# A transformer block with a mixture of experts: the experts' feed-forward in two halves of 1792 columns instead of four quarters of 896

## The chip, the cores and the metric

The kernel runs on one core of one Trainium2 chip. The metric is the device time of one execution in microseconds (us). Five engines matter: TensorE (PE, with the weight loads shown as PEld), VectorE (DVE), ScalarE (ACT), GpSimd (POOL) and SyncE (SP), which issues the loads of the weights. All work in fp32, with products split in two parts.

## The reference

Two layers over 272 tokens (16 of them learned) with 1024 features: a mixer of pooling and differential attention, then a feed-forward. The first layer's feed-forward is dense, the second's a mixture of eight experts, of which each token goes to two:

```python
D_MODEL = 1024; SEQ = 256; D_FF = 3584; N_EXPERTS = 8; TOP_K = 2
def swiglu(h, wg, wu, wd):
    return (jax.nn.silu(h @ wg) * (h @ wu)) @ wd
def moe_swiglu(h, router, wg, wu, wd):
    ...
    out = jnp.zeros_like(h)
    for e in range(N_EXPERTS):
        out = out + combine[..., e:e + 1] * swiglu(h, wg[e], wu[e], wd[e])
    return out
```

After it come the residual and a last norm. Each expert's three matrices are 1024 x 3584, 1024 x 3584 and 3584 x 1024 floats, 44 MB; eight experts make 352 MB of weights that are read once.

## The kernel before, in words

**Dense part.** Until about 615 us the kernel runs the two mixers and the dense feed-forward. The change doesn't touch it.

**Blocks.** The mixture's weights come in blocks of about 1 MB, in the order of use. An expert is worked in `NS` = 4 steps of `SLAB` = 896 columns of the hidden dimension. A step has four blocks of the gate's matrix (256 rows x 896 columns, in SBUF 128 x 2 x 896, 896 KB), four of up's, and four of down's, which belong to the step before: three of 1 MB and one of 512 KB, since 896 rows are seven chunks of 128. `Weights.load` issues them on SP (L101) into raw buffers, as these come free.

**Two parts.** TensorE multiplies at its fast rate in a rounded format; so each block is taken in two parts. ACT copies the upper part, whi (`first_parts`, L149), three blocks ahead of use (`AHEAD`), into one of `NHI` = 7 slots. DVE subtracts it from the block, which gives wlo (`second_parts`, L157), one block ahead (two near the end), into one of `NLO` = 5 slots; with this the raw buffer is free and SP starts the next transfer. PE multiplies both parts with the tokens (`stream`, L1089): eight matmuls a block, 448 columns wide for gate and up, 512 for down.

**Tokens.** An expert has 128 places for tokens. With at most 64 tokens, the tokens' own lower parts lie in the other 64 places, and a fold at the end of each sum (`folded`: ACT copies the sum to part, L1060, and PE multiplies it with fold back into the sum, L1064) adds the two halves. With more than 64, the places are tokens, and the tokens' lower parts are multiplied in extra matmuls behind each pair of blocks (`unit`, under `tc.If(many > 0)`; L1185 for gate and up with exl, L1205 for down with hl).

**A step.** `up(E, "pgate")` sums the gate; after the second block of up the hook `gated` folds it and takes the Silu on ACT (L1210, L1212, gs). `up(E, "pup")` sums up; after the second block of down `product` folds it and multiplies on DVE (L1214, L1216). `down` multiplies the step before into y. `turn` transposes gs on PE (L1072, L1075), ACT copies it to hh (L1266), and `parts_of` makes hl on DVE (L1079, L1081). Hooks, `then(m, f)`, run f behind block m. PE's, ACT's and DVE's order is that of the code (`tc.manual_schedule`); a queue passes nothing.

**PSUM.** y has a pair of banks. All other sums rotate over three pairs.

**The end.** After an expert, `keep` scales y (ACT, L1095, yout) and POOL stores it to `ydram` (L1096). `rows(t)` gathers each token's two rows from `ydram` on POOL (L1136, into yout and exl), and DVE adds them to hsum (L1139). `rows(0)` is called at the end of the last expert's second step, its adds follow six blocks later.

Of the kernel before, what the change touches and what calls it, by code (L numbers as in the profile page):

```python
# [60 lines left out]
class Weights:  # L61
# [3 lines left out]
    def __init__(self, nc, blocks, slots):  # L65
        self.nc, self.blocks = nc, blocks
        self.free = []
        self.kept, self.keep = [], 0
        self.slots = slots
        self.raw = {}  # L70
        self.parts = {}
        self.order = [(b, i) for b, blk in enumerate(blocks) for i in range(blk[1])]
        self.n_split = 0
        self.n_load = 0
        self.first = next(b for b, blk in enumerate(blocks) if blk[2] is None)
        self.n_large = len(blocks) - self.first
        self.n_small = sum(blk[1] for blk in blocks[:self.first])
        self.n_hi = self.n_lo = 0
        self.his, self.los = {}, {}
        self.taken = 0  # L80
        self.second = None
# [63 lines left out]
    def first_parts(self, j):  # L145
        while self.n_hi < min(j + 1, self.n_large):
            w, shaped = self.large(self.n_hi)
            hi = shaped(self.slot(self.n_hi % NHI, f"whi{self.n_hi}"))
            self.nc.scalar.activation(hi, w, AF.Copy)  # L149
            self.his[self.n_hi] = hi  # L150
            self.n_hi += 1

    def second_parts(self, j):
        while self.n_lo < min(j + 1, self.n_large):
            w, shaped = self.large(self.n_lo)
            lo = shaped(self.slot(NHI + self.n_lo % NLO, f"wlo{self.n_lo}"))
            self.nc.vector.tensor_sub(lo, w, self.his[self.n_lo].bitcast(F32))  # L157
            self.los[self.n_lo] = lo
            self.freed(self.first + self.n_lo)
            self.n_lo += 1  # L160
# [3 lines left out]
def tile_block(ctx, tc, x, meta_tokens, rel_bias, w_in, pool_group_w, w_pool_up, w_attn_up, w_out, dense_w_gate,  # L164
# [68 lines left out]
    def add_up(w, e, s):  # L233
        for b in range(4):
            src = w[0, e, b * 256:b * 256 + 256, s * SLAB:(s + 1) * SLAB]
            blocks.append((src.rearrange("(k p) f -> p k f", p=P), 1, None))

    def add_down(e, s, c0, m):
        for b in range((NSC + 1) // 2):
            r = s * SLAB + b * 256  # L240
            n = min(2, NSC - 2 * b)
            src = moe_w_down[0, e, r:r + n * P, c0:c0 + m]
            blocks.append((src.rearrange("(p k) f -> p k f", k=n), 1, None))
# [724 lines left out]
    def places():  # L968
        nc.vector.scalar_tensor_tensor(posb, few[:, None].to_broadcast([P, 2, NE]), float(HALF), pos, op0=ALU.mult,
                                       op1=ALU.add)  # L970

    def tables(pc_):
# [4 lines left out]
        nc.vector.tensor_scalar(big2, few, -1.0, 1.0, op0=ALU.mult, op1=ALU.add)  # L977
# [24 lines left out]
    exl = act.tile([P, 2, NCH, CAP], F32R, name="exl", tag="xl")  # L1002

    class Expert:


        def __init__(self, e):
# [9 lines left out]
            self.xh, self.xl = exh[:, e % 2], exl[:, e % 2]  # L1017
# [5 lines left out]
        def gather(self, cs=range(NCH)):  # L1023
            if cs[0] == 0:
                self.pg = two("pgat").rearrange("p h (c s) -> p (h c) s", s=CAP)
# [5 lines left out]
        def first(self, cs=slice(0, NCH)):  # L1031
            nc.scalar.activation(self.xh[:, cs], self.pg[:, cs], AF.Copy)

# [6 lines left out]
        def scales(self):  # L1040
            self.pst = bank("pst")
# [13 lines left out]
    def folded(E, ps):  # L1055
# [6 lines left out]
        def add():  # L1062
            for hf in range(2):
# [3 lines left out]
    def chunk(ci):  # L1067

        b, i = ci // 2, ci % 2
        return slice(b * 256 + i, (b + 1) * 256, 2) if ci < NSC - 1 else slice(b * 256, SLAB)  # L1070

    def turn(hs):  # L1072
        pt = two("pth").rearrange("p h (c s) -> p (h c) s", s=P)[:, 0:NSC]
        for ci in range(NSC):
            nc.tensor.transpose(pt[:, ci], hs[:, chunk(ci)], ident)  # L1075
        return pt
# [77 lines left out]
    def unit(bs, run, extra, many):  # L1154

        held = []
        m0 = step[0]
        for b in bs:
            m = step[0]
            ws.first_parts(m + AHEAD)  # L1160
            ws.second_parts(m + (1 if m < ws.n_large - 10 else 2))
            held.append(ws.his.pop(m))
            run(b, (held[-1], ws.los.pop(m)))
            if b != bs[-1]:
                for f in hooks.pop(m, ()):
                    f()
                step[0] += 1
        with tc.If(many > 0):  # L1168
            for b, hi in zip(bs, held):
                extra(b, hi)  # L1170
        for f in hooks.pop(step[0], ()):
            f()
        step[0] += 1

    def up(E, name):
        ps = two(name)
        outs = [(ps[:, hf, 0:SW], slice(hf * SW, (hf + 1) * SW)) for hf in range(2)]

        def run(b, parts):
            stream(outs, parts, [E.xh[:, 2 * b], E.xh[:, 2 * b + 1]], b == 0, b == 3)  # L1180

        def extra(b, hi):
            for i in range(2):
                for o, f in outs:
                    nc.tensor.matmul(o, E.xl[:, 2 * b + i], hi[:, i, f], start=False, stop=True, skip_group_check=True)  # L1185

        for bs in ((0, 1), (2, 3)):
            unit(bs, run, extra, E.many)
        return ps[:, :, 0:SW]

    def down(E, s, h, hfs=(0, 1)):
# [4 lines left out]
        def chunks(b):  # L1196
            return range(2 * b, min(2 * b + 2, NSC))

        def run(b, parts):
            stream(outs, parts, [h[0][:, ci] for ci in chunks(b)], s == 0 and b == 0, s == NS - 1 and b == 3)  # L1200

        def extra(b, hi):
            for i, ci in enumerate(chunks(b)):
                for o, f in outs:
                    nc.tensor.matmul(o, h[1][:, ci], hi[:, i, f], start=False, stop=True, skip_group_check=True)  # L1205

        for bs in ((0, 1), (2, 3)):
            unit(bs, run, extra, E.many)

    def gated(E, pg_, gs2, add):  # L1210
        add()
        nc.scalar.activation(gs2, pg_, AF.Silu, scale=E.rc[:, 0:1])  # L1212

    def product(E, pu, gs2, add):  # L1214
        add()
        nc.vector.scalar_tensor_tensor(gs2, pu, E.rc[:, 0:1], gs2, op0=ALU.mult, op1=ALU.mult)  # L1216
# [7 lines left out]
    for e in range(NE):  # L1224
        for s in range(NS):
            end = e == NE - 1 and s == NS - 1
            m0 = step[0]
# [8 lines left out]
            pg_ = up(E, "pgate")  # L1236
            gs = mb.tile([P, SLAB], F32, name="gs")
            gs2 = gs.rearrange("p (h f) -> p h f", h=2)
            add_g = folded(E, pg_)
            then(m0 + 5, lambda E=E, pg_=pg_, gs2=gs2, add=add_g: gated(E, pg_, gs2, add))  # L1240
            pu = up(E, "pup")
            add_u = folded(E, pu)
            if prev is None:
                product(E, pu, gs2, add_u)
            else:
                then(m0 + (8 if end else 9), lambda E=E, pu=pu, gs2=gs2, add=add_u: product(E, pu, gs2, add))
                if end:
                    hh, hl = (x_[:, NE % 2, 0:NSC] for x_ in (exh, exl))

                    def last_turn():  # L1250
                        pt = turn(gs)
                        nc.scalar.activation(hh, pt, AF.Copy)
                        then(m0 + 10, lambda: parts_of(E, pt, hh, hl))

                    then(m0 + 9, last_turn)
                down(prev[0], prev[1], turned)
            if end:
                turned = (hh, hl)
                continue

            m1 = step[0]
            add_y = folded(prev[0], prev[0].y) if prev is not None and prev[1] == NS - 1 else None
            pt = turn(gs)
            hh = mb.tile([P, NSC, P], F32R, name="hh")
            hl = mb.tile([P, NSC, P], F32R, name="hl")
            nc.scalar.activation(hh, pt, AF.Copy)  # L1266
            turned = (hh, hl)
            then(m1, lambda E=E, pt=pt, hh=hh, hl=hl: parts_of(E, pt, hh, hl))
            if add_y is not None:
                then(m1, add_y)  # L1270
                then(m1 + 1, lambda E=prev[0]: keep(E, E.e))
            if e + 1 < NE:
                if s == 0:
                    then(m1 + 4, lambda e=e: (made.append(Expert(e + 1)), made[-1].folds()))
                elif s == 1:
                    made[-1].gather()
                    then(m1, made[-1].first)
                    then(m1 + 1, made[-1].second)
                elif s == 2:
                    made[-1].scales()  # L1280
                    then(m1, made[-1].scaled)
            elif s == 0:
                hsum = residual()
            elif s == 1:
                add = rows(0)
                then(m1 + 5, lambda add=add: (add(), added.append(rows(1))))
                then(m1 + 12, lambda: added[0]())
# [8 lines left out]
    def squares_of(t, hf):  # L1296
        sq = mb.tile([P, SLAB], F32, name="fsq", tag=("gs", "hh")[hf])[:, 0:512]
# [59 lines left out]
    with tc.If(most > CAP):  # L1357
        with tc.For_i(0, NE, 1) as ev:
# [29 lines left out]
            for j in range(NFB):  # L1388
# [26 lines left out]
                ho = mb.tile([P, SLAB], F32, name="ho", tag="hh")[:, 0:512]  # L1415
# [49 lines left out]
```

## Time and profile before

| | us |
|---|---|
| three runs | 1563.52, 1564.65, 1564.68 |
| median | 1564.65 |
| profiled execution, time | 1566.1 |
| profiled execution, span | 1564.3 |
| PE busy in it | 1469.2 (94%) |
| PE weight loads busy | 1277.6 (82%) |
| DVE busy | 1306.1 (83%) |
| ACT busy | 1072.1 (69%) |
| POOL busy | 20.2 (1%) |

The queue of the weights moves 449.97 MB in 177,328 packets. The busy shares are means over the whole span; the mixture, from about 616 us on, has to be read by stretches. A line such as "x4" in the timeline joins four instructions in a row; a matmul's end overlaps the next one's start, so the pace of PE is read from the distance of the starts. The bracket at a row's end tells how long the engine was idle before it and what released it.

### The profile page before, as it was taken

How to read it: one execution, taken by the hardware profiler on the slowest of the kernel's cores; microseconds unless marked ns; L12 is line 12 of the kernel's file. 1: busy time of each engine (PE TensorE's matmuls, PEld its weight loads, DVE VectorE, ACT ScalarE, POOL GpSimd, SP SyncE). 2: the span in 40 equal slices, each digit the busy share in tenths (PEclk: the TensorE clock that was granted, in tenths of full speed). 3: DMA queues.
4: the chain of work that ended last, by engine and by line, in shares of the span. 5: the costliest groups of instructions: out<-in, count | busy, mean ns of one | idle time of the engine just before them, and what ended most of it. 6: DMA issues, size and time to landing. Idle time of an engine off the chain costs nothing. (4 is left out here: it accounts for less than half of the span.)

```text
span 1564.3 us, 22760 instructions
## 1 busy us (share of the span) xinstructions
PE 1469.2 (94%) x8667; PEld 1277.6 (82%) x8667; DVE 1306.1 (83%) x1429; ACT 1072.1 (69%) x1067; POOL 20.2 (1%) x27
## 2 busy tenths in 40 slices
PE   8999999999999997899899999999999999998785
PEld 7989999999999997677677888888776677676563
DVE  7766776666678677799999988878999999999896
ACT  5455554444455645878888767866888888887875
POOL 1000000000000000000000000000000000000100
PEclk9999999999999998999999999999999999999988
DMA  9734454555564336799999999999999999999994
GB/s 307 244 129 136 162 189 169 182 168 183 165 193 136 126 118 237 252 386 409 407 408 408 386 317 355 362 329 331 390 405 410 408 407 409 408 407 405 394 401 152
DMA packets 181266, 460.98 MB, mean 295 GB/s; under 512 B 10378, under 2 KB 83256, under 8 KB 169240
## 3 DMA queue, kind: packets, MB, share of 16 engines
q1 hardware_dynamic: 177328, 449.97, 77.5%
q0 software_dynamic: 2688, 9.24, 1.5%
q8 instruction: 81, 1.33, 0.3%
q14 instruction: 41, 0.34, 0.1%
q10 hardware_dynamic: 1128, 0.11, 0.1%
HBM read 453.49 MB, written 5.80 MB: 294 GB/s over the span
## 5 line engine op out<-in xcount | busy, mean ns | idle before, releaser
L157 DVE TENSOR_TENSOR wlo<-raw,whi 128x1792 fp32r<-128x1792 f32 (+2 forms) x388 | 753.1, 2001 | 28.0 <-ACT whi L149 25.1
L149 ACT ACTIVATE whi<-raw 128x1792 fp32r<-128x1792 f32 (+2 forms) x388 | 639.6, 1681 | 81.4 <-DMA raw<-in_moe_w_gate_dram 28.4
L125 ACT ACTIVATE w<-raw 128x1024 fp32r<-128x1024 f32 x180 | 189.7, 1058 | 251.1 <-PE ps L440 185.4
L126 DVE TENSOR_TENSOR w<-raw,w 128x1024 fp32r<-128x1024 f32 x180 | 219.5, 1223 | 66.4 <-ACT w L125 66.0
L440 PE MATMUL ps<-xh,w 128*128 128x272 f32 (+1 forms) x896 | 177.0, 293 | 0.5 <-ACT hT L761 0.5
L440 PE MATMUL ps<-fh,w 128*128 128x272 f32 x864 | 164.5, 290 | 0.0
L1089 PE MATMUL pgate<-wlo,exh 128*128 128x448 f32 x512 | 132.9, 382 | 22.5 <-DVE wlo L157 21.8
L440 PEld LDWEIGHTS ps<-xh,w 128*128 128x128 f32 x896 | 142.4, 190 | 4.2 <-PE s L502 1.1
L1089 PE MATMUL pgate<-whi,exh 128*128 128x448 f32 x512 | 133.0, 382 | 5.3 <-DVE exh L1036 1.8
L440 PEld LDWEIGHTS ps<-fh,w 128*128 128x128 f32 x864 | 135.7, 188 | 0.0
L1089 PE MATMUL pup<-whi,exh 128*128 128x448 f32 x512 | 127.8, 371 | 7.1 <-PEq L1168 6.0
L1089 PE MATMUL y<-wlo,hh 128*128 128x512 f32 x434 | 127.1, 408 | 6.8 <-DVE wlo L157 3.5
L1089 PEld LDWEIGHTS pgate<-wlo,exh 128*128 128x128 f32 x512 | 95.7, 193 | 44.6 <-DVE wlo L157 37.2
L1089 PE MATMUL pup<-wlo,exh 128*128 128x448 f32 x512 | 127.8, 371 | 2.2 <-DVE wlo L157 2.0
L440 PE MATMUL ps<-xl,w 128*128 128x272 f32 (+1 forms) x448 | 126.8, 288 | 0.0
L1089 PE MATMUL y<-whi,hh 128*128 128x512 f32 x434 | 122.8, 399 | 4.2 <-PEq L1168 1.5
L440 PE MATMUL ps<-fl,w 128*128 128x272 f32 x432 | 124.2, 288 | 0.0
L1089 PEld LDWEIGHTS pup<-whi,exh 128*128 128x128 f32 x512 | 95.0, 189 | 23.4 <-issue 13.7
L1089 PEld LDWEIGHTS y<-wlo,hh 128*128 128x128 f32 x434 | 77.0, 188 | 44.7 <-DVE wlo L157 30.0
L1089 PEld LDWEIGHTS pgate<-whi,exh 128*128 128x128 f32 x512 | 94.5, 193 | 20.9 <-issue 11.0
L1089 PEld LDWEIGHTS pup<-wlo,exh 128*128 128x128 f32 x512 | 93.5, 188 | 17.8 <-DVE wlo L157 10.3
L1089 PEld LDWEIGHTS y<-whi,hh 128*128 128x128 f32 x434 | 79.6, 188 | 27.3 <-issue 6.1
(315 smaller groups left out, 1995.3 us busy)
## 6 DMA issues: line engine op xcount, KB each, us to landing
raw<-in_moe_w_gate_dram SPq DMA_DIRECT2D x128, 896.0 KB, 8.9
raw<-in_moe_w_up_dram SPq DMA_DIRECT2D x128, 896.0 KB, 9.4
raw<-in_moe_w_down_dram SPq DMA_DIRECT2D x93, 1024.0 KB, 9.4
raw<-in_w_in_dram SPq DMA_DIRECT2D x30, 1024.0 KB, 6.3
raw<-in_moe_w_down_dram SPq DMA_DIRECT2D x37, 512.0 KB, 7.9
raw<-in_dense_w_gate_dram SPq DMA_DIRECT2D x14, 1024.0 KB, 5.0
raw<-in_dense_w_up_dram SPq DMA_DIRECT2D x14, 1024.0 KB, 4.9
raw<-in_dense_w_down_dram SPq DMA_DIRECT2D x14, 1024.0 KB, 5.0
```

The lines of the kernel that those rows point to most:

```text
L125: self.nc.scalar.activation(hi, w, AF.Copy)
L126: self.nc.vector.tensor_sub(lo, w, hi.bitcast(F32))
L149: self.nc.scalar.activation(hi, w, AF.Copy)
L157: self.nc.vector.tensor_sub(lo, w, self.his[self.n_lo].bitcast(F32))
L440: newest[0] = nc.tensor.matmul(ps, w_[part][:, k, ms_], xp[:, k, sl], start=t == 0 and k == 0, stop=t == 2 and k == nk - 1).ins
L1089: nc.tensor.matmul(ps, x_, part[:, i, f], start=first and i == 0 and part is parts[0], stop=last and i == len(chunks) - 1 and part is part ...
```

## The change

`NS` becomes 2 and a slab 1792 columns, in four slices (`SW` = 448). A step now has eight blocks of the gate and eight of up, each of 128 rows x 1792 columns (128 x 1 x 1792, still 896 KB, in runs of 7168 contiguous bytes in place of 3584), and seven of down, all of 1 MB. The gate and up have two pairs of banks each (pgate0, pgate1, pup0, pup1). y and the three rotating pairs stay, so pup1 takes the pair that pgate0 had, and the next expert's gather (pnext) that of pgate1.

The first two blocks of up are therefore run in another order: both blocks for pup0's columns, with the fold of pgate0 and its Silu in two halves between them, then both blocks for pup1's. pgate1 is folded and gated after up's fourth block. The product comes in two halves (behind the first and third block of down), the turn in parts of six and eight chunks. `second_parts` runs two blocks ahead all the time, into `NLO` = 4 slots. The next expert's places, gather and scales move to the end of up. In the last step `rows(0)` is called behind the third block of the gate, its adds and `rows(1)` behind the eighth, the second adds behind the twelfth.

A set of blocks that are used whole is prepared for (`whole`, `exf`), but no block is in it: every entry of the list of blocks has a 1 where a whole one would have a 0. What stays of it is two small copies an expert on ACT (exf, 128 x 64).

```diff
-NS = 4
+NS = 2
-NRAW, NRAWE, NPAIR, NHI, NLO, AHEAD = 6, 2, 5, 7, 5, 3
+NRAW, NRAWE, NPAIR, NHI, NLO, AHEAD = 6, 2, 5, 7, 4, 3
-SLAB = DFF // 4
-SW = SLAB // 2
+SLAB = DFF // 2
+SW = SLAB // 4
+NDB = NSC // 2
+NCA = 6
...
     def add_up(w, e, s):
-        for b in range(4):
-            src = w[0, e, b * 256:b * 256 + 256, s * SLAB:(s + 1) * SLAB]
+        for b in range(NCH):
+            src = w[0, e, b * P:(b + 1) * P, s * SLAB:(s + 1) * SLAB]
...
-    def unit(bs, run, extra, many):
+    def unit(bs, runs, extra, many):
...
             ws.first_parts(m + AHEAD)
-            ws.second_parts(m + (1 if m < ws.n_large - 10 else 2))
+            ws.second_parts(m + 2)
...
+        for b in range(0, NCH, 2):
+            runs = [lambda b, parts: block(b, parts, outs)]
+            if b == 0 and between is not None:
+                def some(os, i):
+                    return lambda bs, held: block(bs[i], held[i], os)
...
+                runs = [some(outs[0:2], 0), call(between[0]), some(outs[0:2], 1), call(between[1])]
+                for o in outs[2:4]:
+                    runs += [some([o], 0), some([o], 1)]
+            unit((b, b + 1), runs, extra, E.many)
...
-    def gated(E, pg_, gs2, add):
+    def gated(E, ps, gs2, add, hfs=(0, 1)):
+        add(hfs)
+        hf = slice(hfs[0], hfs[-1] + 1)
+        nc.scalar.activation(gs2[:, hf], ps[:, hf, 0:SW], AF.Silu, scale=E.rc[:, 0:1])
...
+            mg = step[0]
+            mu, md = mg + NCH, mg + 2 * NCH
+            mt = md + (NDB if prev is not None else 0)
...
+            if end:
+
+                then(mg + 2, lambda: added.append(rows(0)))
+                then(mg + 7, lambda: (added[0](), added.append(rows(1))))
+                then(mg + 11, lambda: added[1]())
+            pg_ = [two("pgate0"), two("pgate1")]
+            up(E, sums(pg_[0], 0) + sums(pg_[1], 1))
...
+            pu = [two("pup0"), two("pup1")]
+            add_g = folded(E, pg_[0][:, :, 0:SW])
+
+            def first_gate(E=E, ps=pg_[0], gs2=gs2[0], add=add_g):
+                for hf in range(2):
+                    gated(E, ps, gs2, add, (hf,))
...
+            then(mu + 1, part_g)
+            up(E, sums(pu[0], 0) + sums(pu[1], 1), (first_gate, lambda: None))
+            add_u = folded(E, pu[0][:, :, 0:SW])
+
+            extra_pair = two("pnext")
...
+                then(md, first_product)
+            turns = [(range(0, NCA), "a"), (range(NCA, NSC), "b")]
...
+                if prev[1] == NS - 1:
+                    add_y = folded(prev[0], prev[0].y)
+                    then(mt + 1, add_y)
+                    then(mt + 2, lambda E=prev[0]: keep(E, E.e))
```

The order on the engines, at three places. In these rows a number behind a name tells tiles apart, and a row joins equal instructions in a row.

On ACT, from the end of the gate to up in an expert in the middle, before (pgate and gs are the whole gate of a step, raw the blocks as loaded):

```order
L149 ACTIVATE whi_9021<-raw_8926 128x1792
L1060 ACTIVATE part<-pgate 128x2x448
L1168 UNCONDITIONAL_BRANCH
L149 ACTIVATE whi_9048<-raw_8940 128x1792
L149 ACTIVATE whi_9062<-raw_8972 128x2048
L1212 ACTIVATE gs<-pgate,rcs 128x896
```

and in the change (pgate_8400 and pgate_8401 are the gate's two pairs):

```order
L154 ACTIVATE whi_8534<-raw_8422 128x1792
L1193 UNCONDITIONAL_BRANCH
L1070 ACTIVATE part<-pgate_8400 128x2x448
L154 ACTIVATE whi_8562<-raw_8447 128x1792
L154 ACTIVATE whi_8568<-raw_8463 128x1792
L1254 ACTIVATE gs<-pgate_8400,rcs 128x448 x2
L1070 ACTIVATE part<-pgate_8401 128x2x448
```

The place of the Silu behind part and two upper parts is the same; it is in two halves now, and the second pair's part follows it.

On PE at the same place, before (up's first two blocks, its extras, then the gate's fold):

```order
L1089 MATMUL pup<-whi_7975,exh 128x448 x4
L1089 MATMUL pup<-wlo_8014,exh 128x448 x4
L1089 MATMUL pup<-whi_7998,exh 128x448 x4
L1089 MATMUL pup<-wlo_8041,exh 128x448 x4
L1168 COMPARE_AND_BRANCH
L1185 MATMUL pup<-whi_7975,exl 128x448 x4
L1185 MATMUL pup<-whi_7998,exl 128x448 x4
L1168 UNCONDITIONAL_BRANCH x2
L1064 MATMUL pgate<-part,fold 128x448 x2
```

and in the change (pup_8046 is up's first pair, pup_8047 the second, pgate_7893 the gate's first):

```order
L1099 MATMUL pup_8046<-whi_7985,exh 128x448 x2
L1099 MATMUL pup_8046<-wlo_8010,exh 128x448 x2
L1074 MATMUL pgate_7893<-part,fold 128x448 x2
L1099 MATMUL pup_8046<-whi_8008,exh 128x448 x2
L1099 MATMUL pup_8046<-wlo_8024,exh 128x448 x2
L1099 MATMUL pup_8047<-whi_7985,exh 128x448
L1099 MATMUL pup_8047<-wlo_8010,exh 128x448
L1099 MATMUL pup_8047<-whi_8008,exh 128x448
L1099 MATMUL pup_8047<-wlo_8024,exh 128x448
```

The fold has moved from behind the two blocks and their extras to behind four matmuls, and four more matmuls stand between it and the first on up's second pair.

On DVE in the last step, the adds of the gathered rows in the change (the first wlo is of the block whose upper part, whi_14415, stands just ahead of yout on ACT):

```order
L163 TENSOR_TENSOR wlo_14435<-raw_14304,whi_14415 128x1792
L163 TENSOR_TENSOR wlo_14458<-raw_14320,whi_14433 128x1792
L1193 UNCONDITIONAL_BRANCH
L163 TENSOR_TENSOR wlo_14472<-raw_14343,whi_14456 128x1792
L1193 UNCONDITIONAL_BRANCH
L163 TENSOR_TENSOR wlo_14495<-raw_14378,whi_14470 128x1792
L163 TENSOR_TENSOR wlo_14509<-raw_14394,whi_14493 128x1792
L1193 UNCONDITIONAL_BRANCH
L1149 TENSOR_TENSOR hsum<-hsum,yout 128x1024
L1149 TENSOR_TENSOR hsum<-hsum,exl 128x1024
```

The first adds stand five lower parts behind that block; before, some 17 lower parts stood between, and the second ones now come four lower parts after these.

## Rows read from the trace of the kernel before

**Rows 1.** Windows: us; PE, PEld, DVE, ACT, POOL busy; PEclk, DMA share, GB/s
```profile
640.00:835.00 195.00, 179.70 (x815) 138.52 (x816) 192.10 (x124) 166.78 (x118) 0.55 (x1) 0.99 0.99 388
835.00:1117.00 282.00, 279.45 (x1352) 242.40 (x1351) 239.55 (x150) 211.01 (x149) 1.06 (x2) 1.00 0.95 354
1117.00:1420.00 303.00, 279.81 (x1275) 214.88 (x1273) 298.00 (x192) 264.11 (x188) 2.31 (x4) 1.00 1.02 407
1420.00:1545.00 125.00, 102.95 (x418) 76.30 (x416) 114.46 (x71) 96.62 (x72) 9.63 (x5) 0.95 0.97 375
```

**Rows 2.** Groups of DVE by form, 640 to 835: busy, mean ns; idle before
```profile
L157 DVE TENSOR_TENSOR wlo<-raw,whi 128x1792 fp32r<-128x1792 f32 x57 | 111.9, 2020 | 0.0
L157 DVE TENSOR_TENSOR wlo<-raw,whi 128x2048 fp32r<-128x2048 f32 x21 | 47.0, 2288 | 0.4 <-ACT whi L149 0.3
...
L157 DVE TENSOR_TENSOR wlo<-raw,whi 128x1024 fp32r<-128x1024 f32 x7 | 8.5, 1215 | 0.0
```

**Rows 3.** SP's waits, 640 to 835 (total, times, longest); a row of ACT's timeline
```profile
SPq L101 <- DVE wlo L157: 165.6, 86, 7.4
702.65 1.70 ACT L149 ACTIVATE whi<-raw 128x1792 fp32r<-128x1792 f32 x1 [0.57 <-DMA raw<-in_moe_w_up_dram]
```

**Rows 4.** Line L1185's matmuls (ns min/median/max; first, last start)
```profile
L1185 PE MATMUL pgate<-whi,exl x128: 362/365/369, 835.8 to 1068.6; 128*128 128x448 f32 x128
```

**Rows 5.** PE's timeline at a gate's end with many tokens: start, us
```profile
968.62 1.78 PE L1185 MATMUL pgate<-whi,exl 128*128 128x448 f32 x8
970.24 0.97 PE L1089 MATMUL pup<-whi,exh 128*128 128x448 f32 x4
971.05 0.97 PE L1089 MATMUL pup<-wlo,exh 128*128 128x448 f32 x4
971.87 0.97 PE L1089 MATMUL pup<-whi,exh 128*128 128x448 f32 x4
...
975.11 0.57 PE L1064 MATMUL pgate<-part,fold 128*128 128x448 f32 x2
975.52 0.98 PE L1089 MATMUL pup<-whi,exh 128*128 128x448 f32 x4
```

**Rows 6.** ACT's timeline at the same place
```profile
970.44 0.92 ACT L1060 ACTIVATE part<-pgate 128x896 fp32r<-128x896 f32 x1 [2.46 <-PE pgate L1185]
971.26 3.50 ACT L149 ACTIVATE whi<-raw 128x1792 fp32r<-128x1792 f32 x2
975.72 1.01 ACT L1212 ACTIVATE gs<-pgate,rcs 128x896 f32<-128x896 f32 x1 [0.97 <-PE pgate L1064]
```

**Rows 7.** PE's timeline after gaps; PE's windows (us, busy, PEclk, DMA, GB/s)
```profile
1423.69 1.08 PE L1089 MATMUL pgate<-wlo,exh 128*128 128x448 f32 x4 [2.18 <-DVE wlo L157]
1484.67 1.86 PE L1089 MATMUL pgate<-wlo,exh 128*128 128x448 f32 x4 [2.86 <-DVE wlo L157]
1515.50 1.86 PE L1089 MATMUL pgate<-wlo,exh 128*128 128x448 f32 x4 [3.53 <-DVE wlo L157]
1423.70:1427.00 3.30, 2.95 (x12) 1.00 1.03 411
1484.70:1489.80 5.10, 4.81 (x12) 0.50 1.03 412
```

**Rows 8.** DVE's timeline at the mixture's start
```profile
631.29 3.96 DVE L157 TENSOR_TENSOR wlo<-raw,whi 128x1792 fp32r<-128x1792 f32 x2 [3.57 <-ACT whi L149]
639.98 1.15 DVE L1216 SCALAR_TENSOR_TENSOR gs<-pup,rcs,gs 128x896 f32<-128x896 f32 x1 [4.73 <-PE pup L1064]
```

**Rows 9.** Timelines of ACT, POOL, DVE in the last expert; a DMA issue (landing)
```profile
1453.33 1.11 ACT L1095 ACTIVATE yout<-y,rcs 128x1024 f32<-128x1024 f32 x1
1464.35 3.07 POOL L1136 DMA_INDIRECT yout<-ydram,rows_of  x1 [9.06 <-DMA ydram<-yout]
1467.72 2.58 POOL L1136 DMA_INDIRECT exl<-ydram,rows_of  x1 [0.30 <-issue]
exl<-ydram,rows_of POOLq DMA_INDIRECT x2, 9.0
1492.27 1.22 DVE L1139 TENSOR_TENSOR hsum<-hsum,yout 128x1024 f32<-128x1024 f32 x1
```

More of the change, by code (lines that the diff above doesn't have):

```diff
@@ L77, in __init__ @@
         self.n_small = sum(blk[1] for blk in blocks[:self.first])
+        self.whole = {j for j, blk in enumerate(blocks[self.first:]) if blk[1] == 0}
+        self.parted = [j for j in range(self.n_large) if j not in self.whole]
         self.n_hi = self.n_lo = 0
@@ L1069, in chunk, with turn @@
         b, i = ci // 2, ci % 2
[L1070 to L1075, printed above, removed]
+        return slice(b * 256 + i, (b + 1) * 256, 2)
+    def turn(hs, cis):
+        pt = two("pth").rearrange("p h (c s) -> p (h c) s", s=P)[:, 0:len(cis)]
+        for i, ci in enumerate(cis):
+            nc.tensor.transpose(pt[:, i], hs[:, chunk(ci)], ident)
         return pt
@@ new lines, in unit @@
+            if m in ws.whole:
+                held.append((ws.large(m)[0], None))
+            else:
+                held.append((ws.his.pop(m), ws.los.pop(m)))
+            if len(runs) == 1:
+                runs[0](b, held[-1])
+                if m in ws.whole:
+                    ws.freed(ws.first + m)
+                if b != bs[-1]:
+                    for f in hooks.pop(m, ()):
+                        f()
+        if len(runs) > 1:
+            for run in runs:
+                run(bs, held)
+            for i in range(len(bs)):
+                if m0 + i in ws.whole:
+                    ws.freed(ws.first + m0 + i)
+                if i < len(bs) - 1:
+                    for f in hooks.pop(m0 + i, ()):
+                        f()
@@ L1191, in down, with sums @@
+    def sums(ps, i):
+        return [(ps[:, hf, 0:SW], slice((2 * i + hf) * SW, (2 * i + hf + 1) * SW)) for hf in range(2)]
     def down(E, s, h, hfs=(0, 1)):
@@ L1257, in tile_block @@
[L1257 to L1268, printed above, removed]
@@ L1269, in tile_block @@
-            if add_y is not None:
-                then(m1, add_y)
-                then(m1 + 1, lambda E=prev[0]: keep(E, E.e))
+            if s == NS - 1 and e + 1 < NE:
+                then(mg + 3, made[-1].folds)
+            if end:
[4 more added lines that the diff above has]
+            up(E, sums(pg_[0], 0) + sums(pg_[1], 1))
@@ new lines, in tile_block, with turn_part @@
+            if prev is None:
+                first_product()
+                for f in hooks.pop(md, ()) + hooks.pop(md + 1, []) + hooks.pop(md + 2, []):
+                    f()
+            else:
+                then(md, first_product)
+            turns = [(range(0, NCA), "a"), (range(NCA, NSC), "b")]
+            parts = [None, None]
+            def turn_part(i, at, E=E, gs=gs, end=end, parts=parts):
+                cis, name = turns[i]
+                if end and i == 1:
+                    hh, hl = exh[:, NE % 2], exl[:, NE % 2]
+                else:
+                    hh = mb.tile([P, len(cis), P], F32R, name=f"hh{name}")
+                    hl = mb.tile([P, len(cis), P], F32R, name=f"hl{name}")
+                parts[i] = (hh, hl)
+                pt = turn(gs, cis)
+                nc.scalar.activation(hh, pt, AF.Copy)
+                then(at, lambda: parts_of(E, pt, hh, hl))
@@ L1288, in tile_block @@
+            turned = parts
             prev = (E, s)
```

174 lines of the change are left out of this document (85 added, 89 removed).

## The prediction

> **What bounds the kernel now.** I read first the busy time by stretch of the mixture (the windows), then VectorE's groups of the first stretch, then what SP and ScalarE wait for, then the chain gate to up on PE and ACT, and last the end of the last expert. Everything before 616 us is the same in both kernels, so only the mixture counts.
>
> The four stretches [rows 1] show two regimes. From 640 to 835 and from 1117 to 1420 DVE is busy 192.10 of 195 and 298.00 of 303 us: 2.9 and 5.0 us idle. Its work is the lower part of each block (57 of 2020 ns and 21 of 2288 ns [rows 2]). SP waits for little else: 165.6 us, 86 times, for wlo [rows 3], because a raw buffer comes free only when wlo has read it. ACT meets each block just after it lands, 0.57 us late [rows 3]. So VectorE and the transfers (share 0.99 and 1.02) tie there, and PE, 180 of 195, follows.
>
> From 835 to 1117 it is PE: 279.45 of 282, with DVE idle 42.4 us and ACT 71 [rows 1]. Two experts have more than 64 tokens and run the extra products: L1185 starts 128 times for the gate, which is 2 experts x 4 steps x 16 matmuls [rows 4]. A gap in PE there goes to the end at its full length, since DVE, ACT and the transfers all have slack that PE's time can't use.
>
> The last stretch, 1420 to 1545, has DVE idle 10.5 of 125 us, PE at a mean clock of 0.95 [rows 1].
>
> **Gate to up with many tokens.** Before, the next sum has a bank pair of its own. PE goes from the last extra of the gate (starting 968.62) straight on with up at 970.24, and the fold of the gate comes at 975.11 [rows 5]; the Silu, 975.72, delays nobody [rows 6]. In the change, four sums are live and three pairs rotate, so the upper half of up takes the pair that the gate's first half is in, and PE may not begin it before both Silus of that half have read it. On ACT they stand behind part and two whi. I count from the end T of the gate's extras: 0.2 until ACT starts, part 0.92, two whi 3.50 less their overlap with it, about 3.3 [rows 6], two half Silus, together the whole one's 1.01 and a little more, 1.1, and 0.2 back to PE: T + 5.6 us. PE has for itself until then one half block (four matmuls, 0.81 by the distance of the starts 970.24 and 971.05 [rows 5]), the fold after part (0.4, from 975.11 to 975.52) and another half block, 0.81, with part's end as the only hold: about T + 2.6. **Pause 3.0 us.** There are 2 experts x 2 halves = 4 such boundaries: 12 us.
>
> Then the clock. After gaps of 2.86 and 3.53 us PE's matmuls come at half pace (1.86 for four), after one of 2.18 they don't [rows 7]. After the 2.86 gap the granted clock over 1484.70 to 1489.80 is 0.50, the 1.2 GHz level, and 12 matmuls take 5.10 where three groups at 0.81 take 2.4; after 2.18 it is 1.00, 2.4 GHz [rows 7]. That is about 2.5 us more per pause. 3.0 us lies at the edge, so I count two to three of the four: +6. **Together +18**; ends +10 (the Silus 0.5 earlier, no half clock) and +22 (all four at half clock).
>
> Here a rule speaks another way. The rows show PE busy 279.45 of 282, and PEld, the weight loads, only 242.40 [rows 1]. The Trainium skill, page "Perfetto Trace Analysis", section "Identifying the Most-Contended Engine", holds matmul busy time for a bad measure because matmuls are pipelined, and takes the load row as the better one; by it this stretch would have 14% of room, 39.6 us, and swallow 12 us of pauses. The row on the pace decides for me: four matmuls follow four at 0.81 us through the whole boundary [rows 5], with nothing between them to give back. The same page, section "Matmuls", says that independent groups should rotate through different PSUM banks so that one's evacuation overlaps the next one's matmuls; it speaks against this change, and no run here shows yet what breaking it costs.
>
> **Few tokens (640 to 835, 1117 to 1420, most of 1420 on).** VectorE's work per expert: 32 blocks of 896 KB stay (32 x 2.02). For down, 12 x 2.288 + 4 x 1.215 = 32.3 becomes 14 x 2.288 = 32.0 [rows 2]: -0.3 us an expert. The products (L1216) and hl (L1079) keep their elements. So what larger blocks and longer runs save the transfers can come out only as DVE's idle time, 2.9 + 5.0 us, plus the 0.3 times five experts: at most -9. Against it stands the same boundary. PE follows DVE there, so at T the lower parts of all four blocks from mu on are still to be written, into four slots: 4 x 2.02, less the 0.8 that PE needed for the block before, is T + 7.3. The Silus end at T + 5.6 as above if the two blocks ahead of them have landed, and eight matmuls (1.6) then free the first slot: T + 7.2, just in time. With the 0.57 us by which a block keeps ACT waiting [rows 3], twice, it is T + 8.3, and DVE waits 1 us. I take **-4**, about half of the gain; ends -9 and +8 (1 us at 9 boundaries, and of the gain only the 1.5 of DVE's work). A full stall is a rival.
>
> Neutral: the 16 added copies (two small ones an expert) lie in ACT's idle time, over 28 us in each stretch [rows 1]; at the price of part of a half Silu, at most 0.5 each, they would cost 8 us if that cover were gone. PE's products, folds, turns and gathers are equal in number, and so are the two extras' branches (24 units an expert in both). PE's turns come in two parts, DVE's products and hl as well, with the same elements; a fixed cost more for each lies behind DVE's or PE's slack.
>
> **Start of the mixture.** DVE waits 3.57 us for whi at 631.29 and 4.73 for the first product at 639.98 [rows 8]. With halves the first product comes after 16 blocks in place of 8, when the buffers are full, and nothing waits for its turn: **-2**, ends -5 and +3 (the product's wait merely moves).
>
> **Last expert: the gathered rows.** Before, yout runs at 1453.33, the gathers start on POOL at 1464.35 and 1467.72, and the second lands 9.0 us after: 1476.7, so 23.4 us after yout's start; the adds come only at 1492.27 [rows 9]. In the change the adds stand five wlo (5 x 2.02 = 10.1, with the running one 11) behind the block at which yout runs. **DVE then waits 11 to 12 us**, and SP behind it for buffers. The second gathers wait for the first adds (yout's tile) and are due four wlo, 8.1 us, later; two issues and 9.0 us of landing take about 11: 3 more. 14 to 15 in all, against the 10.5 us that DVE is idle in this stretch anyway [rows 1], which full buffers behind the wait give back: **+4**, ends -6 (the wait hidden) and +14 (nothing given back).
>
> **Sum:** 18 - 4 - 2 + 4 = +16 on the profiled execution's 1566.1 us (span 1564.3): 1582.1. That execution lies 1.45 above the median of the runs, 1564.65, so 1580.7: **1581 us**. 0.2%, 3 us, is about what a measurement of this kernel can tell from no change. With the terms' ends not all at one side, the forecast's own range is 1568 to 1598.
>
> **Rivals.**
> A, faster: PE's pauses don't come out. Either ACT has part and both whi done earlier than PE asks, or PE after a pause runs its waiting work faster than 0.81 for four, as the weight-load row would allow. Then DVE's idle time remains: -7.9, -3 and -2, in all -13: 1552 us. For it: PEld's 242.40 of 282 [rows 1]; the reading that the Trainium skill's page "Perfetto Trace Analysis" gives of such rows stands above. Against it: the pace in rows 5.
> B, about the same: pauses without half clock, +12, and the whole gain elsewhere, -8, -2 and -2: 1565 us. For it: 2.18 us left the clock at 1.00 [rows 7].
> C, much slower: the boundaries with few tokens stall too. It decides from the point where the Silus end after T + 5.7: then DVE has no slot, frees no buffer, and SP starts no transfer, so that the next block is late too. ACT's 0.57 us wait for each landing [rows 3] comes before the Silu, and DVE, the bound, loses some 2.5 us (the 0.57 and one more wlo of 2.02 that comes late) at 9 of the 12 other boundaries (not the first two nor the last, where DVE has idle time): +22 in place of -4, 1607 us. Against it: PE's idle time of 15 us in the first stretch [rows 1] lets it catch up behind a Silu that is late.
>
> **Chances.** Forecast 0.62 (all of it slower by over 3 us), A 0.17, B 0.11 (0.09 within, 0.02 above), C 0.10. Faster 0.17, same 0.09, slower 0.74. The range: 1556 to 1606 takes in the forecast's own, B, a part of A and C's lower half; outside are most of A's low side and C's top, under 0.2.
>
> **What would show it.** Right: between 835 and 1117 four PE gaps near 3 us before the first pup matmul of the upper half, released by ACT's half Silu (gs), half-pace groups after some of them, and the stretch 12 to 22 longer; DVE idle under 8 us in the few-token stretches; near the end DVE waiting about 11 us at the first hsum add for a transfer, released later than wlo. Wrong, if PE passes the boundary without a gap (A), if gates and ups with few tokens show DVE idle of 2 us before wlo released by PE (C), or if the last stretch isn't longer.

## The result and the profile after

The changed kernel takes 1660.33 us (median of four runs, 1657.56 to 1662.02) against 1564.19: the ratio is 1.0613, with an interval of 1.0595 to 1.0632. So it is slower by 96 us, where 16 were forecast; the direction was right and the time lies far outside the range.

The page's busy times after, by engine:

```profile
PE 1501.7 (91%) x8667; PEld 1312.2 (79%) x8667; DVE 1304.6 (79%) x1416; ACT 1069.0 (65%) x1086; POOL 20.4 (1%) x27
```

The span is 1655.8 us, 91.5 more. DVE's work is 1.5 us less than before and ACT's 3.1, so neither got more to do. PE has the same 8667 matmuls and is busy 32.5 us longer (1501.7 less 1469.2): it ran them slower. The mean granted clock from 616 us to the end is 0.94, where it was 0.98. The other 59.0 are idle time of PE.

To see where, I cut both traces at the starts of experts (the first matmul of their gate). Windows of the kernel before: experts 1 and 2, then 3 and 4 (many tokens), 5 to 7, and the last with the end. Columns as in [rows 1].

```profile
616.50:832.50 216.00, 196.09 (x887) 151.90 (x887) 201.50 (x142) 175.24 (x125) 1.05 (x2) 0.98 0.93 363
832.50:1090.40 257.90, 256.62 (x1257) 225.01 (x1255) 217.06 (x138) 190.46 (x135) 1.06 (x2) 1.00 0.95 353
1090.40:1416.80 326.40, 301.94 (x1368) 231.65 (x1367) 320.76 (x204) 284.52 (x201) 1.59 (x3) 1.00 1.02 404
1416.80:1564.30 147.50, 111.59 (x453) 82.21 (x451) 125.33 (x88) 105.39 (x87) 10.35 (x6) 0.92 0.86 334
```

The same four pieces of the changed kernel:

```profile
615.90:849.80 233.90, 199.42 (x857) 159.48 (x858) 194.62 (x137) 168.54 (x126) 1.05 (x2) 0.91 0.87 329
849.80:1126.40 276.60, 261.38 (x1243) 227.26 (x1242) 220.38 (x135) 189.45 (x138) 1.07 (x2) 0.98 0.89 331
1126.40:1491.60 365.20, 317.00 (x1383) 250.88 (x1382) 316.99 (x196) 283.83 (x208) 1.59 (x3) 0.94 0.94 362
1491.60:1655.80 164.20, 120.60 (x481) 87.67 (x479) 133.03 (x92) 110.43 (x92) 10.54 (x6) 0.91 0.82 311
```

The pieces are 17.9, 18.7, 38.8 and 16.7 us longer. Many tokens cost what was forecast (18). Few tokens did not gain 4 us: the three experts of the third piece lost 13 us each. In 1126.40 to 1491.60 DVE is idle 48.2 us (365.20 less 316.99), where it was 5.6 of 326.40, and the granted clock is 0.94 instead of 1.00.

What was waited for in the mixture of the changed kernel (us in total, times, longest):

```profile
ACT gs L1254 <- PE pgate L1074: 91.4, 32, 9.7
DVE wlo L163 <- ACT whi L154: 81.3, 34, 4.6
PE pgate L1074 <- ACT gs L1254: 55.5, 16, 4.7
...
DVE gs L1258 <- PE pup L1074: 36.9, 11, 5.9
...
DVE wlo L163 <- PE pup L1099: 21.4, 5, 4.7
...
PE pnext L1034 <- DVE s L1019: 14.3, 6, 2.9
...
DVE hsum L1149 <- DMA yout<-ydram,rows_of: 8.7, 1, 8.7
```

PE and ACT wait for one another at the gate: the Silu for the fold, 32 times, and the fold for the Silu, 16 times. The kernel before has 10.4 us in 18 waits of the first kind and none of the second.

One boundary from gate to up in an expert with few tokens, on PE (start, us):

```profile
1206.74 0.99 PE L1099 MATMUL pgate<-wlo,exh 128*128 128x448 f32 x4
1208.03 0.65 PE L1099 MATMUL pup<-whi,exh 128*128 128x448 f32 x2 [0.30 <-PEq L1193]
1208.51 0.57 PE L1099 MATMUL pup<-wlo,exh 128*128 128x448 f32 x2
1209.43 0.47 PE L1074 MATMUL pgate<-part,fold 128*128 128x448 f32 x1 [0.34 <-ACT part L1070]
1213.87 0.74 PE L1074 MATMUL pgate<-part,fold 128*128 128x448 f32 x1 [3.98 <-ACT gs L1254]
1214.41 0.95 PE L1099 MATMUL pup<-whi,exh 128*128 128x448 f32 x2
...
1217.78 0.57 PE L1099 MATMUL pup<-wlo,exh 128*128 128x448 f32 x1
```

and on ACT:

```profile
1208.46 0.91 ACT L1070 ACTIVATE part<-pgate 128x896 fp32r<-128x896 f32 x1
1209.26 1.70 ACT L154 ACTIVATE whi<-raw 128x1792 fp32r<-128x1792 f32 x1
1211.60 1.70 ACT L154 ACTIVATE whi<-raw 128x1792 fp32r<-128x1792 f32 x1 [0.64 <-DMA raw<-in_moe_w_up_dram]
1213.20 0.62 ACT L1254 ACTIVATE gs<-pgate,rcs 128x448 f32<-128x448 f32 x1
1214.65 0.64 ACT L1254 ACTIVATE gs<-pgate,rcs 128x448 f32<-128x448 f32 x1 [0.83 <-PE pgate L1074]
1215.19 0.91 ACT L1070 ACTIVATE part<-pgate 128x896 fp32r<-128x896 f32 x1
1215.98 3.28 ACT L154 ACTIVATE whi<-raw 128x1792 fp32r<-128x1792 f32 x2
1223.80 1.01 ACT L1254 ACTIVATE gs<-pgate,rcs 128x896 f32<-128x896 f32 x1 [4.54 <-PE pgate L1074]
```

and on DVE:

```profile
1218.44 5.89 DVE L163 TENSOR_TENSOR wlo<-raw,whi 128x1792 fp32r<-128x1792 f32 x3 [4.29 <-ACT whi L154]
1226.44 8.63 DVE L163 TENSOR_TENSOR wlo<-raw,whi 128x1792 fp32r<-128x1792 f32 x4 [2.10 <-ACT whi L154]
```

The rows read as one chain. The code folds and gates by halves: fold, Silu, fold, Silu. The second fold waits for the first Silu, though it writes the other bank of the pair than the one that this Silu reads; and the Silu stands behind two upper parts. PE stops at 1209.9, with the half block of up that I had counted as its own work still behind that fold. It resumes 4 us later, at half pace, does the second fold, the rest of both blocks and two more blocks, and only then the second pair's fold. DVE, the bound, is stopped twice, and the first row of the two has to be read with care. It puts the 4.29 us down to an upper part, but that part, the first of the two at 1215.98, is done at 1217.68. DVE starts at 1218.44, just after PE's last matmul on the first lower part of up (1217.78 + 0.57 = 1218.35): it waits for that part's slot. The trace's record of DVE's queue says so too: it stands waiting for PE from 1211.55 to 1218.40. The second wait, 2.10 us, does end with an upper part: ACT, in order, stands 4.54 us at the second pair's Silu, and no upper parts are made meanwhile. With DVE's waits in the two wlo rows above (81.3 and 21.4 us) sorted in this way, 15 with 54.3 us end with a slot and 24 with 48.4 us with an upper part. With many tokens the gap at the second fold is 3.22 us long:

```profile
871.75 0.43 PE L1074 MATMUL pgate<-part,fold 128*128 128x448 f32 x1
875.39 0.74 PE L1074 MATMUL pgate<-part,fold 128*128 128x448 f32 x1 [3.22 <-ACT gs L1254]
...
886.00 0.57 PE L1074 MATMUL pgate<-part,fold 128*128 128x448 f32 x2
```

### The profile page after: what moved, and what is told of

It reads as the page before. It is cut to its first block, busy times and chain, and to the rows that moved or that the text cites. A ratio compares the mean times of both kernels' runs of the same rounds, so it can differ in the third digit from the quotient of the medians.

```text
span 1655.8 us, 22750 instructions
## 1 busy us (share of the span) xinstructions
PE 1501.7 (91%) x8667; PEld 1312.2 (79%) x8667; DVE 1304.6 (79%) x1416; ACT 1069.0 (65%) x1086; POOL 20.4 (1%) x27
## 3 DMA queue, kind: packets, MB, share of 16 engines
q1 hardware_dynamic: 143712, 449.97, 74.4%
## 5 line engine op out<-in xcount | busy, mean ns | idle before, releaser
L154 ACT ACTIVATE whi<-raw 128x1792 fp32r<-128x1792 f32 (+2 forms) x375 | 626.9, 1730 | 56.5 <-DMA raw<-in_moe_w_up_dram 21.8
L1099 PE MATMUL pup<-whi,exh 128*128 128x448 f32 x512 | 155.4, 406 | 6.1 <-PEq L1193 1.7
L1099 PE MATMUL pup<-wlo,exh 128*128 128x448 f32 x512 | 153.0, 401 | 6.0 <-DVE wlo L163 5.7
L1099 PEld LDWEIGHTS pup<-whi,exh 128*128 128x128 f32 x512 | 106.0, 213 | 29.9 <-issue 17.6
L1099 PEld LDWEIGHTS pup<-wlo,exh 128*128 128x128 f32 x512 | 107.0, 211 | 20.3 <-DVE wlo L163 9.6
L1254 ACT ACTIVATE gs<-pgate,rcs 128x448 f32<-128x448 f32 (+1 forms) x48 | 36.3, 757 | 91.4 <-PE pgate L1074 91.4
L445 PE MATMUL ps<-hh,w 128*128 128x272 f32 x448 | 85.7, 290 | 0.0
L445 PEld LDWEIGHTS ps<-xl,w 128*128 128x128 f32 x448 | 84.2, 190 | 0.7 <-issue 0.4
L1074 PE MATMUL pgate<-part,fold 128*128 128x448 f32 x64 | 27.7, 473 | 60.7 <-ACT gs L1254 55.5
```

Of the source, the lines that this page charges most:

```text
L445: newest[0] = nc.tensor.matmul(ps, w_[part][:, k, ms_], xp[:, k, sl], start=t == 0 and k == 0, stop=t == 2 and k == nk - 1).ins
L1074: nc.tensor.matmul(ps[:, hf], E.fold, part[:, hf, 0:n], start=False, stop=True, skip_group_check=True)
L1099: nc.tensor.matmul(ps, x_, part[:, i, f], start=first and i == 0 and part is parts[0], stop=last and i == len(chunks) - 1 and part is part ...
L1254: nc.scalar.activation(gs2[:, hf], ps[:, hf, 0:SW], AF.Silu, scale=E.rc[:, 0:1])
```

## The experiments

Theory M is this chain. Its rivals: H, only the split into halves hurts; O, the loss is not the gate's, but that of the larger halves, the four slots and the late products. All times are medians; ratios go against the kernel before on the same chip.

**e1_fold_pair.** One fold of both banks and one Silu.

```diff
-                for hf in range(2):
-                    gated(E, ps, gs2, add, (hf,))
+                gated(E, ps, gs2, add)
```

> The changed kernel with the first gate pair folded in one piece and one Silu of 896, in place of fold, half Silu, fold, half Silu. Theory M (order of the chain: PE stops at the second fold because it waits for the first half Silu, which stands behind two upper parts on ACT): PE's gap at the fold goes, but PE then waits for the Silu before up's second pair, after one half block more; each of 16 boundaries gets about 2 us shorter: 1620 to 1640 us. Theory H (only the split into halves hurts): 1580 or less. Theory O (four lo slots, halves as large, products late; the gate's chain doesn't matter): 1650 to 1665.

1636.73 us, ratio 1.0478 (1.0455 to 1.0501): 24 us less than the change, as M had it. The fold no longer stops PE, and the first matmul on the gate's old banks does:

```profile
1249.20 0.57 PE L1074 MATMUL pgate<-part,fold 128*128 128x448 f32 x2
1249.60 0.57 PE L1099 MATMUL pup<-whi,exh 128*128 128x448 f32 x2
1250.62 0.67 PE L1099 MATMUL pup<-wlo,exh 128*128 128x448 f32 x2 [0.44 <-DVE wlo L163]
1252.99 0.48 PE L1099 MATMUL pup<-whi,exh 128*128 128x448 f32 x1 [1.70 <-ACT gs L1254]
1253.31 0.37 PE L1099 MATMUL pup<-wlo,exh 128*128 128x448 f32 x1
```

This is the boundary that the prediction had drawn. H falls: 73 of the 96 us are still there.

**e2_silu_early.** The halves stay; in up's first unit the two upper parts (and the lower parts with them in the code) come behind the two Silus.

```diff
+            if len(runs) == 1:
-            ws.first_parts(m + AHEAD)
-            ws.second_parts(m + 2)
+                ws.first_parts(m + AHEAD)
+                ws.second_parts(m + 2)
...
-            for run in runs:
+            for i, run in enumerate(runs):
                 run(bs, held)
+                if i == 1:
+                    for j in range(len(bs)):
+                        ws.first_parts(m0 + j + AHEAD)
+                        ws.second_parts(m0 + j + 2)
```

> The changed kernel with the two upper parts of up's first unit moved behind the two half Silus on ACT. Theory M: PE's gap at the second fold falls from 3.2 to 4.0 us to about 1, the clock stays at its upper level behind it, the second Silu finds its fold done: 1575 to 1595 us. Theory H: the halves stay, so does most of the loss: 1640 or more. Theory O: 1650 to 1665; the upper parts come later, so DVE may even wait more.

1602.96 us, ratio 1.0254 (1.0237 to 1.0271): 57 us less, short of M's 1575 to 1595 by 8. PE's waits of the fold for the Silu fall from 55.5 to 12.3 us, ACT's for the fold from 91.4 to 35.3. None of DVE's waits before a lower part ends with a slot that up holds any more.

**e3_both.** Both edits.

> Both: one fold and one Silu, and the two upper parts behind it. Theory M: PE's gap at each boundary about 0.5 us, 1560 to 1580 us. Theory O: 1650 or more. If e3 lies no lower than e2, the halves cost nothing once the Silu is early.

1595.61 us, ratio 1.0208 (1.0178 to 1.0237). That is 7 us below e2, but the runs of the two overlap (1596.26 to 1603.64 and 1593.30 to 1601.00), so what the halves alone cost is not clear. Of the fold's waits none is left, and up waits for the Silu 2.2 us in eight times. With many tokens an expert takes 127.9 and 130.7 us, where the kernel before takes 128.0 and 130.0: beside it the three rotating pairs cost next to nothing there any more. O falls as the main cause: the slots, the larger halves and the late products are all still there, and 65 of the 96 us are gone. But M's 1560 to 1580 is missed by 16. The excess is in experts with few tokens, some 114 us each where it was 109, and in the last piece (162.6 us, 147.5 before). For the former the trace has one place, at the end of up in an expert's first half. PE, then DVE:

```profile
1241.83 5.44 PE L1034 MATMUL pnext<-s,h2g 128*128 128x128 f32 x32 [3.60 <-DVE s L1019]
```

```profile
1240.93 0.53 DVE L1019 TENSOR_SCALAR s<-cst,pos,sel 128x64 f32<-128x64 f32 x2
...
1249.66 1.15 DVE L1263 SCALAR_TENSOR_TENSOR gs<-pup,rcs,gs 128x896 f32<-128x896 f32 x1 [5.56 <-PE pup L1074]
```

The places s of the next expert are made on DVE at the end of up, behind the lower parts that run ahead. PE waits for them, gathers at a mean granted clock of 0.69 (1241.80 to 1247.30), and the product waits for PE.

**e4_late_silu.** The change with the second pair's Silu two blocks later on ACT, its fold left in place.

```diff
-                then(mu + 3, lambda: gated(E, ps, gs2, add))
+                then(mu + 3, add)
+                then(mu + 5, lambda: gated(E, ps, gs2, lambda hfs: None))
```

> The changed kernel with only the Silu of the gate's second pair moved two blocks later on ACT, its fold on PE left in place. Theory M's second half (ACT stands still 4.5 to 5.8 us at this Silu until PE folds, the upper parts behind it come late and DVE, the bound with few tokens, waits for them): DVE's wait for upper parts falls, 1600 to 1630 us, with PE's gap at the first fold still 3 to 4 us. If the first gap alone makes the loss: within 10 us of the changed kernel's 1660.

1629.42 us, ratio 1.0425 (1.0407 to 1.0442): 31 us less, with the fold's waits unchanged (53.4 us). So the second half of M holds by itself: ACT standing at that Silu costs a third of the loss. Sorted as above, DVE's waits for upper parts fall from 48.4 to 14.1 us, and those for a slot stay (54.4). In the rows ACT's wait at the Silu is now 0.17 us:

```profile
1253.92 6.91 ACT L154 ACTIVATE whi<-raw 128x1792 fp32r<-128x1792 f32 x4
1261.01 1.01 ACT L1254 ACTIVATE gs<-pgate,rcs 128x896 f32<-128x896 f32 x1 [0.17 <-PE pgate L1074]
```

**e5_places.** e3_both with the places made behind up's fourth block.

```diff
+            if s == 0 and e + 1 < NE:
+                then(mu + 3, lambda e=e: made.append(Expert(e + 1)))
...
-                    made.append(Expert(e + 1))
```

> e3_both with the next expert's places (the four small DVE operations s) made behind up's fourth block instead of at up's end. In e3_both each expert with few tokens still takes about 114 us where it took 109 before, and DVE stands still once for 5.6 to 6.4 us at the first product of an expert's first half, while PE waits 3.6 us for s and then gathers at half pace. Theory M2 (this order makes it): that wait goes, 5 us an expert, seven experts: 1562 to 1575 us. Rival (the gather on PE in front of down makes it, whenever s is ready): PE's 32 gather matmuls still hold the product, 1585 or more.

1568.57 us, ratio 1.0035 (1.0021 to 1.0048): 27 us less than e3_both. Experts with few tokens are back at 107.6 to 109.5 us. At the same place PE gathers without a wait, at a granted clock of 1.00:

```profile
1219.91 3.81 PE L1034 MATMUL pnext<-s,h2g 128*128 128x128 f32 x32
```

**e6_places_rows** and **e7_rows.** The adds of the gathered rows behind blocks 13 and 19 of the last step, on e5_places and on e3_both.

```diff
-                then(mg + 7, lambda: (added[0](), added.append(rows(1))))
-                then(mg + 11, lambda: added[1]())
+                then(mg + 13, lambda: (added[0](), added.append(rows(1))))
+                then(mg + 19, lambda: added[1]())
```

> e5_places with the adds of the gathered rows behind the gate's eighth block plus six (block 13 of the last step) and block 19, the first gathers where they are. In e3_both DVE waits 8.5 and 2.2 us there for the gathers. Theory: 8 to 11 us less than e5_places, so 1552 to 1566 us, level with the kernel before or faster by under 1%. Rival (the wait only takes the place of other idle time of DVE in the last expert, full buffers giving it back): within 3 us of e5_places.

> e3_both with only the adds of the gathered rows moved as in e6_places_rows: 8 to 11 us less than e3_both, 1585 to 1590 us, by the theory; within 3 us of it by the rival.

1564.31 us, ratio 1.0001 (0.9992 to 1.0010), and 1588.61 us, ratio 1.0159 (1.0145 to 1.0173): 4.3 less than e5_places and 7.0 less than e3_both. In e3_both the first adds wait so (DVE):

```profile
1518.37 1.22 DVE L1149 TENSOR_TENSOR hsum<-hsum,yout 128x1024 f32<-128x1024 f32 x1 [8.51 <-DMA yout<-ydram,rows_of]
1521.81 1.23 DVE L1149 TENSOR_TENSOR hsum<-hsum,exl 128x1024 f32<-128x1024 f32 x1 [2.22 <-DMA exl<-ydram,rows_of]
```

Of these 10.7 us four to seven come out at the end, less than the theory's 8 to 11 and more than the rival's 3: neither range held.

**e8_no_gate.** e6's two edits without those of the gate.

> The changed kernel with the next expert's places made earlier and the adds of the gathered rows later (as in e6_places_rows), the gate's chain left as the change has it. Additive parts: 27 us for the places (e3_both to e5_places) and 4 to 7 for the rows less than the change, about 1628 us. Rival (the stops overlap: while ACT stands at the Silu, DVE's other waits cost nothing): 1640 to 1660 us.

1632.23 us, ratio 1.0443 (1.0429 to 1.0457). The two edits take 28 us here, where they took 31 from e3_both to e6_places_rows with the gate mended. So the parts nearly add up, and the rival falls. The gate's chain is worth 65 us (the change to e3_both) to 68 (e8_no_gate to e6_places_rows).

**b1_lo4.** The other side: the kernel before with only the four slots and the lead of two blocks.

```diff
-NRAW, NRAWE, NPAIR, NHI, NLO, AHEAD = 6, 2, 5, 7, 5, 3
+NRAW, NRAWE, NPAIR, NHI, NLO, AHEAD = 6, 2, 5, 7, 4, 3
...
-            ws.second_parts(m + (1 if m < ws.n_large - 10 else 2))
+            ws.second_parts(m + 2)
```

> The kernel before with only the slots of the lower parts cut from five to four and second_parts two blocks ahead throughout, as in the change. Theory M: this part of the change costs little, 1560 to 1572 us. Theory O (four slots are what makes DVE and PE wait on each other): 1580 or more.

1555.08 us, ratio 0.9950 (0.9936 to 0.9963): faster, which I had not expected. In the kernel before, O's slots and lead are thus no cost at all. The change with five slots was not run, so how much of the 54.3 us at slots the fifth would have saved is not shown. Experts 3, 4 and 5 gain 1.1, 1.6 and 3.1 us. The page shows the same number of matmuls, busy 11.8 us less than before:

```profile
PE 1457.4 (94%) x8667; PEld 1282.3 (83%) x8667; DVE 1306.2 (84%) x1429; ACT 1071.2 (69%) x1067; POOL 19.6 (1%) x27
```

**b2_lo5_two, b3_raw8, b4_hi8.** The lead of two with five slots; b1 with the saved slot as an eighth raw buffer; b1 with it as an eighth slot of upper parts and ACT four blocks ahead.

```diff
-                then(3, lambda: ws.open((act, "g", 1)))
+                then(3, lambda: ws.open((act, "g", 1), (wslots[-1][0], "y", 1)))
```

> The kernel before with second_parts two blocks ahead throughout and five slots kept. b1_lo4 was 9 us faster than the kernel before. If the lead of two blocks makes that: 1552 to 1557 us, like b1_lo4 or a little better. If the four slots make it: 1562 to 1566.

> b1_lo4 with the memory of the fifth slot given to an eighth raw buffer. If transfers that wait for a buffer still cost time at the start and in the last expert (DVE waits there for upper parts that wait for landing blocks): 1547 to 1553 us. If VectorE bounds it: within 3 us of b1_lo4's 1555.

> b1_lo4 with that memory given to an eighth slot of upper parts and ACT four blocks ahead. ACT is not the bound and waits for landing blocks, so a longer lead has nothing to take: within 3 us of b1_lo4's 1555, or a little slower, since the Silu stands behind one more upper part.

1556.11 us, ratio 0.9956 (0.9940 to 0.9971); 1551.08 us, 0.9922 (0.9909 to 0.9936); 1555.59 us, 0.9948 (0.9934 to 0.9962). So the lead makes b1's gain, not the fewer slots, and a raw buffer is the better use of the memory. **b3_raw8 beats both kernels**, by 0.8% the one before.

## Why the prediction was wrong

**Gate to up with many tokens: +18 forecast, 18.7 measured, for a reason other than the one drawn.** The step that failed is that PE has for itself the fold "and another half block, 0.81, with part's end as the only hold". The two folds have a Silu between them in the code, and the second fold waits for it. The row of the order that I quoted, fold x2, hides this: it joins two instructions of one engine, and what must happen on another engine in between doesn't appear. The four gaps are 3.22 to 3.23 us against 3.0, but earlier in PE's work. PE's idle time in this piece grows by 13.9 us (15.2 less 1.3; 12 forecast) and its busy time by 4.8 (6 forecast for the clock): the clock falls at all four, at 1.2 us each, where two to three at 2.5 were counted. That the sums agree is luck in part. e1_fold_pair has the boundary as drawn: four gaps of 2.56 to 2.57 us, a lower clock behind two of them, and the two experts together 13.3 us longer than before. (The terms listed for the Silus add up to T + 5.7, not 5.6.) The half clock itself, at the gap with few tokens: over 1213.90 to 1218.90 the granted clock is 0.50, the 1.2 GHz level, and 13 matmuls take 5.00 us, where 14 took 2.60 just before the gap.

```profile
1205.00:1207.60 2.60, 2.60 (x14) 1.00 1.00 403
1213.90:1218.90 5.00, 5.00 (x13) 0.50 1.01 420
```

**Few tokens: -4 forecast, 13 us an expert measured.** This is the term that broke the forecast. The step: "eight matmuls (1.6) then free the first slot: T + 7.2, just in time". At the boundary shown T, the end of the gate, is 1207.73. The second half Silu ends at 1215.29, T + 7.6 in place of T + 5.6, since PE's second fold lies between the two; PE comes out of the gap at half pace with half a block of up's first pair still to do; and the first slot is free at 1218.35, T + 10.6. DVE waits 4.3 us where 1 was allowed for. Such a wait stands at 15 of the 16 boundaries, 54.3 us together. The second stop had no term at all: the second pair's Silu, hook mu+3, holds ACT, which I had taken to run on, until PE has caught up, and the upper parts behind it. In the prediction this Silu has no line; moving it gave 31 us (e4_late_silu).

Rival C had the place (the boundaries with few tokens stall) and, for the first stop, the mechanism (DVE has no slot); its sign, DVE idle by over 2 us before a lower part until PE is done, is there. Its price was 2.5 us at 9 boundaries; e8_no_gate to e6_places_rows gives 68 us for 16, 4.2 each. Its argument against, that PE's idle 15 us would let it catch up, failed too: over the 5 us behind each of the 16 gaps PE's granted clock is only 0.50 to 0.71.

**Gathers "equal in number": 0 forecast, 27 us measured** (e3_both to e5_places). The count was right and the order was left out. Before, the places are made seven blocks ahead of the gather; in the change, on the spot. The moved step was priced by its instructions and not by what stands ahead of it on DVE.

**Start: -2 forecast.** In the changed kernel the first expert takes 111.7 us against 106.6. With the chains mended (e6_places_rows) it takes 97.8, and the last piece 155.1 against 147.5. Most of both can be one shift that I had not seen: a step's down is worked in the next step, so a longer step carries 3.5 blocks more, 3.5 x 2.288 = 8.0 us of DVE's work [rows 2], from the first expert into the last. By this estimate it is zero in sum; no run tests it by itself.

**Last expert: +4 forecast, 4.3 and 7.0 measured** (e6_places_rows, e7_rows), the wait itself 8.5 + 2.2 us (e3_both) where 11 to 12 were counted, and 3 more for the second adds, which found their gathers landed. Right in kind, and the size lies between the forecast's 4 and its end of 14.

**VectorE's work and the longer runs.** DVE's work fell by 1.5 us in all (1304.6 against 1306.1), 0.2 an expert where 0.3 was forecast. Packets of the weights' queue fell from 177,328 to 143,712 and the gate's blocks land 6.3 us after issue in place of 8.9, but with everything mended the kernel is level with the one before: where DVE is the bound, this buys nothing. The fairer comparison is with b1_lo4, which has the change's slots and lead: on the same chip it takes 1555.08 us, the mended change 1564.31. So with these equal the halves are still 9 us slower; 2.8 of it lie in the two experts with many tokens (258.1 against 255.3), and the rest was not traced.

**Rules weighed.** By the Trainium skill, page "Perfetto Trace Analysis", section "Identifying the Most-Contended Engine", the 14% that the weight loads left free should have swallowed the gaps with many tokens. The trace does not agree: 18.7 us came out at the end. The Trainium skill's same page, section "Matmuls", wants independent groups to rotate through different PSUM banks. The runs fit with a condition: with the same banks shared, the Silu behind two upper parts costs 41 us more (e1_fold_pair) than ahead of them (e3_both), and with it ahead an expert with many tokens takes 127.9 and 130.7 us against 128.0 and 130.0 before.

What stays open: why matmuls in b1_lo4 are busy 11.8 us less at the same mean clock (0.986); b2_lo5_two shows that the lead of two blocks makes the gain in time, not how.

## What to carry to other kernels

Where two engines that run in order wait for each other, follow the chain back and forth, and for each wait ask what is queued behind it on the engine that stands still: here 31 of the 96 us went when ACT no longer stood at one Silu ahead of upper parts. A wait that hangs on two engines is put down to one of them; look when each was done. Put the short operation that another engine waits for ahead of bulk work that has a lead anyway; moving the first pair's Silus ahead of two upper parts gave 57 of the 96 us. When a step is moved, compare the position of its inputs on their own queue, not only its price.

## What the runs showed that was not expected

After the gap of 3.98 us PE ran at half clock for 5 us, and 32.5 of the 91.5 us that the span grew are matmuls that were busy longer, in the same number. After e1_fold_pair's gap of 1.70 us the matmuls of 448 columns come 0.21 us apart (1253.31, then 1253.52), so at full pace; after the 3.98 us gap they come 0.37 apart. The length of the gap alone does not tell which: of the four gaps of 2.56 to 2.57 us in e1_fold_pair the granted clock over the next 5 us is 1.00 behind two and 0.66 behind the other two, and it is 0.66 behind one of 2.04 us. A third of such a stop's cost can thus lie behind it, in rows that show no wait at all.
